# The forget gate of a two-layer decoder kernel as eight float32 products on column tiles

## Chip, core and metric

One core of a Trainium2 chip runs the whole kernel. The metric is the device time of one execution in microseconds (us). TensorE (PE) multiplies, VectorE (DVE) and ScalarE (ACT) copy, scale and reduce, GpSimd (POOL) does small things on the side, and SyncE (SP) issues nearly all DMAs. PE's clock has two levels, 1.2 and 2.4 GHz; the granted clock in the rows is a share of the higher one.

## What is computed

Two pre-norm layers over 256 tokens of width 1024: forgetting attention, then block-sparse attention, each followed by a SwiGLU feed-forward part and a gated embedding. The change touches the entry of the first layer:

```python
u = _rmsnorm(h, attn_norm_g[i])
proj = u @ fox_w_in[j]                      # (256, 3 * 1024 + 16)
q, k, v = _heads(proj[..., :D]), _heads(proj[..., D:2 * D]), _heads(proj[..., 2 * D:3 * D])
f_logit = proj[..., 3 * D:].astype(jnp.float32) + fox_b_f[j].astype(jnp.float32)
log_f = jax.nn.log_sigmoid(f_logit).transpose(0, 2, 1)
o = _fox_attention(q, k, v, log_f)          # logits get cumsum(log_f)[t] - cumsum(log_f)[s]
```

The sixteen columns at the end of `proj`, one per head, are the forget gate.

## The kernel before

Every large product is made three times, from operands split into a high part in float32r and the rest: hi by hi, hi by lo, lo by hi (`mm3`, lines 90 to 92). Weights come in tiles of 128 partitions by 1024 columns (512 KB, `half` and `blocks`). Each goes through three steps: SP's DMA into `raw` (six buffers), ACT's copy into `whi` (line 149), DVE's difference into `wlo` (line 150). Then PE uses it in about 2.7 us. The activations are split in the same way by `Norm.block` (line 183 on ACT, 184 on DVE) into `g`, times the norm's gain but without the norm's factor for each token. That factor is applied to the results.

The first layer's attention begins with the value stage (`attention`, loop over `c`): eight weight tiles k = 0 to 7, one for each 128 rows of the width, twelve products of 512 columns each, into four PSUM banks `v`. The first tile is taken in an order of its own (`enter`, line 382), since its halves come in one after the other. Tiles 1 and 2 share a DMA buffer `hw` with pieces of x; the other pieces come in `hw[:, 2]`.

After k = 3 the gate is made (`mid`, that is `fox_bias`): its weights `wf32`, copied four times side by side and split into `fh` and `fl`, take 24 products into the bank `pf`. Then ACT squares the residual in four parts (`square`, line 199), DVE and POOL turn the sums into the factor of each token (`root`, `col`), two products with an identity spread that factor over all partitions (`spread`, line 217, bank `pr`), and ACT and DVE copy it out (lines 220 and 221). ACT also issues three small DMAs here (`small`, line 285). `rest`, which is called behind the value stage, makes the logarithm and the running sum out of `pf`. The later norms call `spread` three more times.

The program is written in the order of the sources and scheduled by the framework: it sets for each engine one fixed order, and semaphores release the instructions in it. Each engine works off its own order.

Some tiles are laid out with gaps (`ENTRY`, `gapped`): where a new group of products begins, either DVE's difference is cut in two pieces or the first block stands apart from the rest.

Of the kernel before, what the change touches and what calls it, by code (L numbers as in the profile page):

```python
# [27 lines left out]
F32 = mybir.dt.float32  # L28
# [4 lines left out]
P = 128  # L33
# [38 lines left out]
def trunk(ctx: ExitStack, tc: tile.TileContext, x, xg, wx, xr, pt, w, cst, gf, rel, hot, rvm, out):  # L72
# [15 lines left out]
    def mm3(o, a, b, start, stop):  # L88
        (ah, al), (bh, bl) = a, b
        mm(o, ah, bh, start=start, stop=False, skip_group_check=True)  # L90
        mm(o, ah, bl, start=False, stop=False, skip_group_check=True)  # L91
        mm(o, al, bh, start=False, stop=stop, skip_group_check=True)  # L92


    first_line = one.tile([P, 32], F32, name="first_line")
# [27 lines left out]
    def half(at=0, entry=0):  # L123


        i = state["next"]
        state["next"] += 1
        if i not in (1, 2):
            raw = work.tile([P, HW + LINE], F32, tag="raw", bufs=RAW, name=f"raw{i}")
        ht, lt = (work.tile([P, HW + 2 * LINE], F32R, tag=n, bufs=6, name=f"{n}{i}") for n in ("whi", "wlo"))  # L130
        hi, lo = ht[:, at:at + HW], lt[:, at:at + HW]
        if entry:
            nc.sync.dma_start(raw[:, 0:HW], w[i - 2][:, 0:HW])
            nc.scalar.activation(hi, raw[:, 0:HW], AF.Copy)  # L134
            ats = [(at + FURTHER, 0, entry), (at + LINE, entry, HW)]
            for a, c0, c1 in ats:
                nc.vector.tensor_tensor(lt[:, a + c0:a + c1], raw[:, c0:c1], f32(hi[:, c0:c1]), op=ALU.subtract)  # L137
            return hi, [lt[:, a + k * P:a + (k + 1) * P] for a, c0, c1 in ats for k in range(c0 // P, c1 // P)]
        if i in (1, 2):
            raw = hw[:, i - 1, S:]  # L140
        parts = 2 if i < 2 else 1
        for q in range(parts):
            c = slice(q * HW // parts, (q + 1) * HW // parts)
            if i in (1, 2):
                at = slice(c.start + (S if q else 0), c.stop + S)
# [26 lines left out]
    class Norm:  # L172
# [39 lines left out]
        def spread(self, scale=1.0):  # L212

            n = self.n
            pr = bank(f"pr{n}")
            for t in range(2):
                mm(pr[:, t * P:(t + 1) * P], self.col[:, t:t + 1].to_broadcast([P, P]), ident,
                   start=True, stop=True)
            self.row = work.tile([P, 2, S], F32, tag="row", name=f"row{n}")
            nc.scalar.activation(self.row[:, 0], pr[:, 0:S], AF.Copy, scale=scale)  # L220
            nc.vector.tensor_copy(self.row[:, 1], pr[:, 0:S])
# [2 lines left out]
            return self.hi[:, m], self.lo[:, m]  # L224

    nm = Norm(0)
    nm.block(0, hx[0])
    first = [half()]
    for k in range(1, 4):
        first.append(half())  # L230
        if k < 3:
            nm.block(k, hx[k])
    nc.sync.dma_start(hw[:, 2], xr)
    for k in range(3, KT):
        nm.block(k, hx[k])
# [25 lines left out]
    def tokens(o, x, t, w, start, stop):  # L261

        at = slice(t * P, (t + 1) * P)
        mm3(o, (x[0][:, at], x[1][:, at]), w, start, stop)

    def pair_unit(bks, c, wt, x, ts=(0, 1), mid=None):

# [14 lines left out]
    def small(after):  # L282
        with tc.issue_after(after.ins):
            for t, a in ((rl, rel), (ht, hot), (rm, rvm)):
                nc.scalar.dma_start(t, a)
        table_parts()


    def fox_bias(nm):

        ft, lt = (work.tile([P, HW + 2 * LINE], F32R, tag=t, bufs=6, name=n) for n, t in (("fh", "whi"), ("fl", "wlo")))

        def four(t, at, k0, k1):
            return t[:, at + k0 * P:at + k1 * P].rearrange("p (k r c) -> p k r c", r=4, c=2 * H)

        n = len(ENTRY)
        fh = four(ft, APART, 0, KT)
        fl = [four(lt, APART + FURTHER, 0, n), four(lt, APART + LINE, n, KT)]  # L300
        for t in (fh, *fl):
            nc.gpsimd.memset(f32(t)[:, :, :, H:], 0.0)
        w4 = wf32.unsqueeze(2).to_broadcast([P, KT, 4, H])
        nc.scalar.activation(fh[:, :, :, 0:H], w4, AF.Copy)
        for t, k0, k1 in ((fl[0], 0, n), (fl[1], n, KT)):
            nc.vector.tensor_tensor(t[:, :, :, 0:H], w4[:, k0:k1], f32(fh[:, k0:k1, :, 0:H]), op=ALU.subtract)
        cols = [[t[:, k].rearrange("p r c -> p (r c)") for t in ts for k in range(t.shape[1])] for ts in ((fh,), fl)]
        pf = bank("pf")
        for k in range(KT):
            mm3(pf[:, :S], [t[k] for t in cols], nm.k(k),  # L310
                start=(k == 0), stop=(k == KT - 1))

        def rest():
            f = one.tile([P, S], F32, name="f")
            nc.vector.tensor_tensor(f, pf[:, :S], nm.row[:, 1], op=ALU.mult)
# [20 lines left out]
            return (lambda i: (mask[:, P:], mask)), add  # L336

        return rest

    def table_parts():  # L340
# [33 lines left out]
        return spread, load, (at, None)  # L374


    def enter(bks, x, w):

        for hf in range(2):
            for a, b in ((0, 0), (1, 0), (0, 1)):  # L380
                for t in range(2):
                    mm(bks[2 * t + hf], x[a][:, t * P:(t + 1) * P], w[b][:, hf * HC:(hf + 1) * HC],
                       start=a == b, stop=False, skip_group_check=True)

    def attention(layer, nm, mid, early, nf):
        vb = [bank(f"v{layer}_{b}") for b in range(4)]
        rest = None
        for c in range(4):
            wt = [early.pop(0) if early else half() for _ in range(2)]
            for kk in range(2):  # L390
                hi, lo = wt[kk]
                k = 2 * c + kk
                if layer == 1 and k == 3:
                    nm.turn(1)
                    nm.square(1)
                if early and k == 0:
                    enter(vb, nm.k(0), wt[0])
                    continue
                for t in range(2):
                    for hf in range(2):  # L400
                        cols = slice(hf * HC, (hf + 1) * HC)
                        tokens(vb[2 * t + hf], nm.k(k), t, (hi[:, cols], lo[:, cols]), k == 0, k == KT - 1)
# [24 lines left out]
        pq = {}  # L427

        def project(j, a):
            if j > 2 and j % 2 == 0 and a == 0:  # L430
# [459 lines left out]
```

## Time and profile before

| what | value |
|---|---|
| median of 3 runs (lowest, highest) | 655.08 us (654.88, 655.27) |
| the profiled execution, its span | 654.99 us, 653.0 us |
| PE busy | 644.5 us, 99% |
| DVE, ACT, POOL busy | 438.7, 376.4, 10.2 us |
| mean share of the DMA engines from 5.4 to 30 us, and after | 0.98 to 1.03, then 0.56 |
| granted PE clock over the span | 0.997 |

The span runs from the first to the last instruction; the run's time has some 2 us around it. A busy PE does not mean that it moves at its best: the ends of matmuls are modelled, so it is the starts that are to be read. Starts that follow each other at the shortest distance mean a full PE.

### The profile page before, as it was taken

The page shows a single profiled execution, that of the slowest core. Times are in us where ns is not written, and L with a number is a line of the kernel's source. Part 1 is how long each engine was busy: PE and PEld are TensorE (multiplying, and loading weights), DVE is VectorE, ACT ScalarE, POOL GpSimd, SP SyncE. Part 2 cuts the span into 40 slices and gives each one's busy share as a digit, 9 for nine tenths or more (in the row PEclk, how much of TensorE's full clock was granted, in tenths as well). Part 3 has the DMA queues.
Part 4 walks back from the last instruction along what each step waited for, and adds up shares of the span by engine and source line. Part 5 has one row for each costly group of instructions (what it writes and reads, how often), then busy time and mean ns, then how long its engine had stood idle before and what let it go on. Part 6 is the DMA issues. An engine that isn't in the chain of part 4 may idle for free.

```text
span 653.0 us, 11639 instructions
## 1 busy us (share of the span) xinstructions
PE 644.5 (99%) x4587; PEld 590.9 (90%) x4587; DVE 438.7 (67%) x717; ACT 376.4 (58%) x654; POOL 10.2 (2%) x24
## 2 busy tenths in 40 slices
PE   9999999999999999999999999999999999999995
PEld 7899988999999999998889999889999999999885
DVE  5788875586666666667675788666666666666665
ACT  7876675664444445448665677756544444454663
POOL 1100000000000000000000000000000000000000
PEclk9999999999999999999999999999999999999998
DMA  9969534286556556565586554344765665665501
GB/s 335 369 231 306 186 126 152 82 266 196 194 186 200 190 189 214 193 191 187 192 291 197 172 174 142 111 148 139 228 194 189 194 197 189 196 209 193 190 0 65
DMA packets 36085, 124.14 MB, mean 190 GB/s; under 512 B 3936, under 2 KB 6208, under 8 KB 36032
## 3 DMA queue, kind: packets, MB, share of 16 engines
q1 hardware_dynamic: 35552, 122.85, 57.3%
q8 instruction: 36, 0.59, 0.3%
q10 hardware_dynamic: 480, 0.55, 0.2%
q14 instruction: 17, 0.14, 0.1%
HBM read 122.32 MB, written 4.22 MB: 194 GB/s over the span
## 4 chain that ended last, share of the span: by engine, by line
PE 95%; issue 3%; DMA 1%; ACT 0%; POOL 0%; DVE 0%; POOLq 0%
PE gu L90 12%; PE gu L91 12%; PE gu L92 12%; PE fo L91 6%; PE fo L90 6%; PE fo L92 6%; PE pq L90 5%; PE pq L91 4%; PE pq L92 4%; PE wo L90 2%; PE wo L92 2%; PE wo L91 2%; PE v L91 2%; PE v L92 2%; PE v L90 2%
## 5 line engine op out<-in xcount | busy, mean ns | idle before, releaser
L150 DVE TENSOR_TENSOR wlo<-raw,whi 128x1024 fp32r<-128x1024 f32 (+1 forms) x187 | 227.4, 1220 | 118.6 <-ACT whi L149 117.0
L149 ACT ACTIVATE whi<-raw 128x1024 fp32r<-128x1024 f32 (+1 forms) x187 | 195.7, 1053 | 143.1 <-PE gu L91 46.2
L90 PE MATMUL gu<-g,whi 128*128 128x256 f32 x704 | 195.2, 277 | 0.0
L92 PE MATMUL gu<-g,wlo 128*128 128x256 f32 x704 | 194.8, 277 | 0.0
L91 PE MATMUL gu<-g,whi 128*128 128x256 f32 x704 | 194.8, 277 | 0.0
L90 PEld LDWEIGHTS gu<-g,whi 128*128 128x128 f32 x704 | 132.2, 188 | 0.8
L91 PEld LDWEIGHTS gu<-g,whi 128*128 128x128 f32 x704 | 132.2, 188 | 0.8
L92 PEld LDWEIGHTS gu<-g,wlo 128*128 128x128 f32 x704 | 132.4, 188 | 0.0
L90 PE MATMUL pq<-g,whi 128*128 128x256 f32 x256 | 71.5, 279 | 0.0
L92 PE MATMUL pq<-g,wlo 128*128 128x256 f32 x256 | 70.9, 277 | 0.0
L91 PE MATMUL pq<-g,whi 128*128 128x256 f32 x256 | 70.9, 277 | 0.0
L90 PE MATMUL fo<-whi,fp 128*128 128x512 f32 x176 | 68.9, 391 | 0.0
L91 PE MATMUL fo<-wlo,fp 128*128 128x512 f32 x176 | 68.7, 390 | 0.0
L92 PE MATMUL fo<-whi,fp 128*128 128x512 f32 x176 | 68.5, 389 | 0.0
L90 PEld LDWEIGHTS pq<-g,whi 128*128 128x128 f32 x256 | 48.1, 188 | 0.6 <-issue 0.2
L92 PEld LDWEIGHTS pq<-g,wlo 128*128 128x128 f32 x256 | 48.2, 188 | 0.0
L91 PEld LDWEIGHTS pq<-g,whi 128*128 128x128 f32 x256 | 48.1, 188 | 0.0
L258 ACT ACTIVATE fp<-sg 128x256 fp32r<-128x256 f32 x44 | 18.2, 418 | 48.5 <-DVE sg L611 48.5
L137 DVE TENSOR_TENSOR wlo<-raw,whi 128x256 fp32r<-128x256 f32 (+1 forms) x40 | 26.1, 688 | 23.7 <-ACT whi L134 23.7
L92 PEld LDWEIGHTS fo<-whi,fp 128*128 128x128 f32 x176 | 33.0, 188 | 7.0
L90 PEld LDWEIGHTS fo<-whi,fp 128*128 128x128 f32 x176 | 33.0, 188 | 6.3
L91 PEld LDWEIGHTS fo<-wlo,fp 128*128 128x128 f32 x176 | 33.0, 188 | 6.0
(156 smaller groups left out, 900.7 us busy)
## 6 DMA issues: line engine op xcount, KB each, us to landing
raw<-w SPq DMA_DIRECT2D x205, 512.0 KB, 3.6
raw<-w SPq DMA_DIRECT2D x8, 540.0 KB, 3.8
d<-d SPq DMA_DIRECT2D x4, 768.0 KB, 9.8
bias<-d SPq DMA_DIRECT2D x4, 512.0 KB, 5.1
h<-x SPq DMA_DIRECT2D x2, 512.0 KB, 9.4
out<-end SPq DMA_DIRECT2D x3, 256.0 KB, 2.0
hw<-wx SPq DMA_DIRECT2D x1, 640.0 KB, 6.5
hw<-xr SPq DMA_DIRECT2D x1, 640.0 KB, 8.3
```

The source lines that it names most:

```text
L90: mm(o, ah, bh, start=start, stop=False, skip_group_check=True)
L91: mm(o, ah, bl, start=False, stop=False, skip_group_check=True)
L92: mm(o, al, bh, start=False, stop=stop, skip_group_check=True)
L137: nc.vector.tensor_tensor(lt[:, a + c0:a + c1], raw[:, c0:c1], f32(hi[:, c0:c1]), op=ALU.subtract)
L149: nc.scalar.activation(hi[:, c], raw[:, c], AF.Copy)
L150: nc.vector.tensor_tensor(lo[:, c], raw[:, c], f32(hi[:, c]), op=ALU.subtract)
L258: nc.scalar.activation(hi, src, AF.Copy)
```

## The change

It makes the gate in float32, without the split: the weights are multiplied by the gain once (`wg`), and each of the eight products takes 32 columns of weights (16 of them zero) against a piece of x as it came in. Product k goes to the 32 partitions (k mod 4) of `pf`, so that four products use four different column tiles of PE, and the second four add to the first. ACT copies the bank out (`quarters`), and one more float32 product with `add4`, ones where rows belong to one head, sums the four quarters into `fsum`. This product and the spreading stand behind k = 5 now. The spreading products become transposes. The first hi copies (the first half of tiles 0 and 1, all of tile 2) go from ACT to DVE, with `nm.block` called inside `half`. `enter` is used for k = 1 too, in another order of its products. In layer 1 one more tile gets its difference in two pieces in place of a gap.

```diff
@@ half
-        for q in range(parts):
-            c = slice(q * HW // parts, (q + 1) * HW // parts)
+        cs = [slice(q * HW // parts, (q + 1) * HW // parts) for q in range(parts)]
+        for c in cs:
...
-            nc.scalar.activation(hi[:, c], raw[:, c], AF.Copy)
+        for c in cs:
+            if i < 3 and c.start == 0:
+                nc.vector.tensor_copy(hi[:, c], raw[:, c])
+                nm.block(i, hx[i])
+            else:
+                nc.scalar.activation(hi[:, c], raw[:, c], AF.Copy)
             nc.vector.tensor_tensor(lo[:, c], raw[:, c], f32(hi[:, c]), op=ALU.subtract)
@@ Norm.spread
-                mm(pr[:, t * P:(t + 1) * P], self.col[:, t:t + 1].to_broadcast([P, P]), ident,
-                   start=True, stop=True)
+                nc.tensor.transpose(pr[:, t * P:(t + 1) * P], self.col[:, t:t + 1].to_broadcast([P, P]), ident)
@@ fox_bias
-        fh = four(ft, APART, 0, KT)
-        fl = [four(lt, APART + FURTHER, 0, n), four(lt, APART + LINE, n, KT)]
...
-        nc.scalar.activation(fh[:, :, :, 0:H], w4, AF.Copy)
...
+        wg = work.tile([P, KT, 2 * H], F32, tag="sg", name="wg")
+        nc.gpsimd.memset(wg[:, :, H:], 0.0)
+        nc.vector.tensor_tensor(wg[:, :, 0:H], wf32, gn[:, 0, :].unsqueeze(2).to_broadcast([P, KT, H]), op=ALU.mult)
+        add4 = work.tile([P, 2 * S], F32, tag="fp", bufs=4, name="add4")[:, 0:P]
+        nc.gpsimd.tensor_copy(add4.rearrange("p (r h) -> p r h", h=H), sel32.unsqueeze(1).to_broadcast([P, P // H, H]))
         pf = bank("pf")
         for k in range(KT):
-            mm3(pf[:, :S], [t[k] for t in cols], nm.k(k),
-                start=(k == 0), stop=(k == KT - 1))
+            at = slice(k % 4 * 32, k % 4 * 32 + 32)
+            mm(pf[at, :S], wg[:, k], hx[k], start=k < 4, stop=k >= 4, skip_group_check=True)
+        quarters = work.tile([P, S], F32, tag="sg", name="quarters")
+        nc.scalar.activation(quarters, pf[:, :S], AF.Copy)
+        pf = []
+
+        def gather():
+            pf.append(bank("fsum"))
+            mm(pf[0][:, :S], add4, quarters, start=True, stop=True)
@@ attention
-                if early and k == 0:
-                    enter(vb, nm.k(0), wt[0])
+                if layer == 0 and k < 2:
+                    enter(vb, nm.k(k), wt[k], k == 0)
...
                 nm.root()
-                nm.spread(-0.125)
                 small(done)
+            if layer == 0 and c == 2:
+                with tc.issue_after(got.ins):
+                    nm.spread(-0.125)
+                    rest.gather()
...
-                hi, lo = blocks(ENTRY if j == 2 * layer and a == 0 else ())
+                hi, lo = blocks(ENTRY if j in ((0,), (2, 4))[layer] and a == 0 else ())
```

PE, behind the last product of k = 3, before (the first three of the gate's 24 products; `pr` spreads the factor, `whi_263` and `wlo_264` are the tile of k = 4):

```order
L92 MATMUL v_3_155<-whi_118,g_87 128x512
L90 MATMUL pf<-g_87,fh 128x256
L91 MATMUL pf<-g_87,fh 128x256
L92 MATMUL pf<-g_87,fl 128x256
...
L217 MATMUL pr_250<-con,col_248 128x128 x2
L90 MATMUL v_0_152<-whi_263,g_87 128x512
L90 MATMUL v_1_153<-whi_263,g_87 128x512
L90 MATMUL v_2_154<-whi_263,g_87 128x512
L90 MATMUL v_3_155<-whi_263,g_87 128x512
L91 MATMUL v_0_152<-wlo_264,g_87 128x512
```

The same place after; `whi_240` and `wlo_241` are the tile of k = 4 now, `whi_246` that of k = 5, `whi_284` that of k = 6:

```order
L92 MATMUL v_3_155<-whi_118,g_87 128x512
L300 MATMUL pf<-gx,wg 32x256
L300 MATMUL pf<-hw,wg 32x256 x7
L90 MATMUL v_0_152<-whi_240,g_87 128x512
L90 MATMUL v_1_153<-whi_240,g_87 128x512
L91 MATMUL v_0_152<-wlo_241,g_87 128x512
...
L92 MATMUL v_3_155<-whi_246,g_87 128x512
L222 MATMUL pr_275<-con,col_231 128x128 x2
L307 MATMUL fsum<-quarters,add_207 128x256
L90 MATMUL v_0_152<-whi_284,g_87 128x512
```

Eight products stand in place of 24, the spreading and the sum come two tiles later, and at k = 4 two products instead of four stand ahead of the first that reads wlo.

ACT, from the squares to the copies of k = 4 and k = 5, before (`sq` are the squares, `rl`, `ht` and `rm` the small DMAs):

```order
L199 ACTIVATE sq_0_1_241,ss_88<-h 128x512
L199 ACTIVATE sq_1_1_243,ss_88<-h 128x512
L285 DMA rl<-rel 64x16
L285 DMA ht<-hot 64x384
L285 DMA rm<-rvm 16x384
L149 ACTIVATE whi_263<-raw_262 128x1024
L149 ACTIVATE whi_269<-raw_268 128x1024
L220 ACTIVATE row_253<-pr_250 128x256
```

ACT at the same place after:

```order
L204 ACTIVATE sq_0_1_224,ss_88<-h 128x512
L302 ACTIVATE quarters<-pf 128x256
L204 ACTIVATE sq_1_1_226,ss_88<-h 128x512
L284 DMA rl<-rel 64x16
L284 DMA ht<-hot 64x384
L284 DMA rm<-rvm 16x384
L154 ACTIVATE whi_240<-raw_239 128x1024
L154 ACTIVATE whi_246<-raw_245 128x1024
```

The copy of the gate's bank, which reads what PE's eight products write, stands ahead of the last square, the DMA issues and the copies for k = 4 and k = 5; the copy of the spread factor no longer stands right behind these.

DVE at the first tiles, before (`whi_110` and `wlo_111` are the tile of k = 2, `wlo_119` that of k = 3):

```order
L150 TENSOR_TENSOR wlo_111<-hw,whi_110 128x1024
L184 SCALAR_TENSOR_TENSOR g_87<-hw,gx,g_87 128x256
L150 TENSOR_TENSOR wlo_119<-raw_117,whi_118 128x1024
L184 SCALAR_TENSOR_TENSOR g_87<-hw,gx,g_87 128x256 x5
```

DVE there after:

```order
L151 CAST whi_110<-hw 128x1024
L189 SCALAR_TENSOR_TENSOR g_87<-hw,gx,g_87 128x256
L155 TENSOR_TENSOR wlo_111<-hw,whi_110 128x1024
L155 TENSOR_TENSOR wlo_119<-raw_117,whi_118 128x1024
L189 SCALAR_TENSOR_TENSOR g_87<-hw,gx,g_87 128x256
```

The copy of tile 2 is DVE's now, and the difference of g comes between it and the difference of the weights.

## Rows read from the trace of the kernel before

**Rows 1.** The page's first section: PE's busy time, share of the span, instructions.

```profile
PE 644.5 (99%) x4587; PEld 590.9 (90%) x4587; DVE 438.7 (67%) x717; ACT 376.4 (58%) x654; POOL 10.2 (2%) x24
```

**Rows 2.** Waits of PE: who waited for whom, us in total, times, longest.

```profile
PE v L382 <- ACT whi L149: 0.7, 1, 0.7
```

**Rows 3.** Timeline at k = 2: start, length, engine, line, operation, out<-in, count.

```profile
9.06 1.06 ACT L149 ACTIVATE whi<-hw 128x1024 fp32r<-128x1024 f32 x1 [0.91 <-DMA hw<-wx]
...
10.16 1.23 DVE L150 TENSOR_TENSOR wlo<-hw,whi 128x1024 fp32r<-128x1024 f32 x1 [1.27 <-ACT whi L149]
...
11.46 0.71 PE L91 MATMUL v<-wlo,g 128*128 128x512 f32 x2
...
12.83 2.07 DVE L184 SCALAR_TENSOR_TENSOR g<-hw,gx,g 128x256 fp32r<-128x256 f32 x5
```

**Rows 4.** Timeline of PE at the gate, and to the start of k = 6.

```profile
16.55 0.28 PE L90 MATMUL pf<-g,fh 128*128 128x256 f32 x1
...
19.31 0.60 PE L217 MATMUL pr<-con,col 128*128 128x128 f32 x4
19.67 1.17 PE L90 MATMUL v<-whi,g 128*128 128x512 f32 x4
20.67 0.39 PE L91 MATMUL v<-wlo,g 128*128 128x512 f32 x1
...
22.49 0.39 PE L90 MATMUL v<-whi,g 128*128 128x512 f32 x1
...
25.21 0.39 PE L90 MATMUL v<-whi,g 128*128 128x512 f32 x1
```

**Rows 5.** Timeline of PE: transposes, then float32 products on 64-column tiles.

```profile
82.77 0.82 PE L497 MATMUL pp<-con,e 128*128 128x128 f32 x6
83.52 1.08 PE L511 MATMUL po<-pt,v 128*64 128x256 f32 x8
84.43 0.61 PE L513 MATMUL po<-pt,v 128*64 128x128 f32 x8
```

**Rows 6.** Timeline of ACT, its DMA issues (ACTq), and one row of DVE.

```profile
0.74 0.41 ACTq L115 DMA_DIRECT2D gx<-xg  x1
...
1.19 1.28 ACT L102 ACT_TABLE_LOAD   x1 [1.19 <-PEq L882]
...
14.91 0.19 ACT L199 ACTIVATION_READ_ACCUMULATOR sq<-h 128x1 f32 x1
...
15.14 0.53 ACTq L285 DMA_DIRECT2D rl<-rel  x1
...
16.30 0.62 ACT L199 ACTIVATE sq<-h 128x512 f32<-128x512 f32 x1
...
16.34 0.60 ACTq L285 DMA_DIRECT2D rm<-rvm  x1
...
16.99 2.02 ACT L149 ACTIVATE whi<-raw 128x1024 fp32r<-128x1024 f32 x2
...
18.09 2.36 DVE L150 TENSOR_TENSOR wlo<-raw,whi 128x1024 fp32r<-128x1024 f32 x2 [0.68 <-ACT whi L149]
...
19.95 0.39 ACT L220 ACTIVATE row<-pr 128x256 f32<-128x256 f32 x1 [0.94 <-PE pr L217]
```

**Rows 7.** Groups by line: the spreading products (busy us, mean ns, idle).

```profile
L217 PE MATMUL pr<-con,col 128*128 128x128 f32 x16 | 2.4, 274 | 0.0
```

**Rows 8.** Timeline at the first products of the feed-forward part's second half.

```profile
137.73 0.76 DVE L259 TENSOR_TENSOR fp<-sg,fp 128x256 fp32r<-128x256 f32 x2
...
139.86 0.39 PE L92 MATMUL fo<-whi,fp 128*128 128x512 f32 x1
```

**Rows 9.** Stretches: length, busy us of each engine, PEclk, DMA share, GB/s.

```profile
0.70:3.85 3.15, 3.08 (x7) 2.51 (x8) 0.00 (x0) 1.49 (x2) 1.35 (x6) 1.00 0.62 187
...
645.70:648.90 3.20, 0.31 (x3) 0.11 (x2) 2.04 (x8) 1.90 (x4) 0.55 (x1) 1.00 0.27 105
...
648.97:653.00 4.03, 0.00 (x0) 0.00 (x0) 0.48 (x1) 0.45 (x1) 0.00 (x0) 0.50 0.44 170
```

More of the change, by code (lines that the diff above doesn't have):

```diff
@@ L91, in mm3 @@
         mm(o, ah, bl, start=False, stop=False, skip_group_check=True)
-        mm(o, al, bh, start=False, stop=stop, skip_group_check=True)
+        return mm(o, al, bh, start=False, stop=stop, skip_group_check=True)
     first_line = one.tile([P, 32], F32, name="first_line")
@@ L141, in half @@
         parts = 2 if i < 2 else 1
-        for q in range(parts):
-            c = slice(q * HW // parts, (q + 1) * HW // parts)
+        cs = [slice(q * HW // parts, (q + 1) * HW // parts) for q in range(parts)]
+        for c in cs:
             if i in (1, 2):
-                at = slice(c.start + (S if q else 0), c.stop + S)
+                at = slice(c.start + (S if c.start else 0), c.stop + S)
                 nc.sync.dma_start(hw[:, i - 1, at], wx[i - 1][:, at])
@@ L226, in trunk @@
     nm = Norm(0)
[L227 to L232, printed above, removed]
+    first = [half() for _ in range(4)]
     nc.sync.dma_start(hw[:, 2], xr)
@@ L263, in tokens @@
         at = slice(t * P, (t + 1) * P)
-        mm3(o, (x[0][:, at], x[1][:, at]), w, start, stop)
+        return mm3(o, (x[0][:, at], x[1][:, at]), w, start, stop)
     def pair_unit(bks, c, wt, x, ts=(0, 1), mid=None):
@@ L289, in fox_bias @@
     def fox_bias(nm):
[L293 to L298, printed above, removed]
-        fh = four(ft, APART, 0, KT)
-        fl = [four(lt, APART + FURTHER, 0, n), four(lt, APART + LINE, n, KT)]
-        for t in (fh, *fl):
-            nc.gpsimd.memset(f32(t)[:, :, :, H:], 0.0)
-        w4 = wf32.unsqueeze(2).to_broadcast([P, KT, 4, H])
-        nc.scalar.activation(fh[:, :, :, 0:H], w4, AF.Copy)
-        for t, k0, k1 in ((fl[0], 0, n), (fl[1], n, KT)):
-            nc.vector.tensor_tensor(t[:, :, :, 0:H], w4[:, k0:k1], f32(fh[:, k0:k1, :, 0:H]), op=ALU.subtract)
-        cols = [[t[:, k].rearrange("p r c -> p (r c)") for t in ts for k in range(t.shape[1])] for ts in ((fh,), fl)]
+        wg = work.tile([P, KT, 2 * H], F32, tag="sg", name="wg")
[3 more added lines that the diff above has]
+        nc.gpsimd.tensor_copy(add4.rearrange("p (r h) -> p r h", h=H), sel32.unsqueeze(1).to_broadcast([P, P // H, H]))
         pf = bank("pf")
         for k in range(KT):
-            mm3(pf[:, :S], [t[k] for t in cols], nm.k(k),
-                start=(k == 0), stop=(k == KT - 1))
+            at = slice(k % 4 * 32, k % 4 * 32 + 32)
[6 more added lines that the diff above has]
+            mm(pf[0][:, :S], add4, quarters, start=True, stop=True)
         def rest():
             f = one.tile([P, S], F32, name="f")
-            nc.vector.tensor_tensor(f, pf[:, :S], nm.row[:, 1], op=ALU.mult)
+            nc.vector.tensor_tensor(f, pf[0][:, :S], nm.row[:, 1], op=ALU.mult)
             nc.vector.tensor_scalar(f, f, bfs, None, op0=ALU.add)
@@ L336, in rest @@
             return (lambda i: (mask[:, P:], mask)), add
+        rest.gather = gather
         return rest
@@ L374, in moba_bias, with enter @@
         return spread, load, (at, None)
[L377 to L383, printed above, removed]
+    def enter(bks, x, w, start):
+        for hf, a, b in [(hf, a, 0) for hf in range(2) for a in range(2)] + [(0, 0, 1), (1, 0, 1)]:
+            for t in range(2):
+                mm(bks[2 * t + hf], x[a][:, t * P:(t + 1) * P], w[b][:, hf * HC:(hf + 1) * HC],
+                   start=start and a == b, stop=False, skip_group_check=True)
     def attention(layer, nm, mid, early, nf):
@@ L401, in attention @@
                         cols = slice(hf * HC, (hf + 1) * HC)
-                        tokens(vb[2 * t + hf], nm.k(k), t, (hi[:, cols], lo[:, cols]), k == 0, k == KT - 1)
+                        got = tokens(vb[2 * t + hf], nm.k(k), t, (hi[:, cols], lo[:, cols]), k == 0, k == KT - 1)
             if layer == 0 and c == 1:
@@ L429, in project @@
         def project(j, a):
-            if j > 2 and j % 2 == 0 and a == 0:
+            if j > 2 + 2 * layer and j % 2 == 0 and a == 0:
                 hi, lo = gapped()
             else:
-                hi, lo = blocks(ENTRY if j == 2 * layer and a == 0 else ())
+                hi, lo = blocks(ENTRY if j in ((0,), (2, 4))[layer] and a == 0 else ())
             if a == 0:
@@ L838 @@
         seq += _rows(wi[:, 2 * D:3 * D])
-        seq += [_gapped(a) if n % 4 == 0 and n > 4 else a for n, a in enumerate(_cols(wi[:, :D], wi[:, D:2 * D]))]
+        seq += [_gapped(a) if n % 4 == 0 and n > 4 + 4 * i else a for n, a in enumerate(_cols(wi[:, :D], wi[:, D:2 * D]))]
         seq += [_wide(wo, 2 * c, hf) for hf, c in ((0, 0), (1, 0), (0, 1), (1, 1), (0, 2), (1, 2), (0, 3), (1, 3))]
```

## The prediction

> **What bounds the kernel now.** I read the page's first section, then what TensorE (PE) waited for, then the order of time of each engine between 4 and 26 us, where the change lies. PE is busy for 644.5 of 653.0 us [rows 1], and in the whole run its products wait for an operand once, before the first product of the value stage [rows 2]. From there on it goes from product to product, one of 512 columns every 0.227 us: eight take the 1.82 us between 20.67 and 22.49 [rows 4]. So a microsecond that PE gains or loses early goes to the end, since nothing later waits and could give it back. The one question is whether the operands still come in time where the products go.
>
> **The change, part by part.** I follow PE through the value stage, whose weight tiles k = 0 to 7 take 12 products each, and give each place as after minus before. The profiled execution took 654.99 us, its span 653.0; the median shown is 655.08, so both bases agree to 0.1 us, and I add to 654.99.
>
> *First tiles.* VectorE (DVE) now makes the first hi copies, so the first product may start up to half a microsecond sooner. That is lost again at k = 2. Its weights land at 9.06, where ScalarE (ACT) begins its copy; DVE's difference follows at 10.16, lasts 1.23, and the first wlo product comes at 11.46 [rows 3], 0.07 behind its end. After, DVE does it all in a row: copy, g difference, wlo. No row has this copy. The nearest are ACT's of the same tile, 1.06 us [rows 3], and DVE's difference over as many columns, 1.13 from one to the next (2.36 - 1.23) [rows 3, 6]; I take 1.13, DVE's own pace. Five g differences take 2.07, 0.41 each [rows 3]. So wlo ends at 9.06 + 1.13 + 0.41 + 1.23 = 11.83 instead of 11.39: **+0.44**. The bounds: a copy as long as one whole difference, 1.23, makes it +0.54; from below, a copy of no length ends wlo at 10.70, PE itself, if it starts at about 5.0 and makes 26 products by then, comes there at 11.0, so -0.5. The Trainium skill (VectorE: DVE Perf Modes, section Mode 2×_2P — use both read ports for one tensor) has it that a float32 copy from SBUF to SBUF takes two elements a cycle. No row here shows that; with about 0.53 for the copy, as an estimate from that page, every sum below would be 0.6 us lower, and the forecast 656.8.
>
> *Gate products.* Before, 24 products fill 16.55 to 19.31 (2.76 us), and the two spreading products come behind them, to 19.67 [rows 4]. After, eight float32 products stand there. A float32 product is two instructions (the two of a spread show as x4). On two 64-column tiles eight such instructions, 256 columns wide, took 0.91 us, from 83.52 to 84.43, and 1.08 to the end of the last [rows 5]: two at a time, 0.23 a round. Four 32-column tiles are not in the trace; four at a time make four rounds and again 1.08, two at a time eight rounds, 0.91 more. I take the first, since tiles of one product each did overlap, plus 0.10 for entering the tiled form. The gate then ends at 16.55 + 0.44 + 0.10 + 1.08 = 18.17. For PE alone this is a gain of about 1.7 us.
>
> *Who waits for that.* ACT's order now has the copy "quarters" of that bank ahead of the last square, three DMA issues and the copies of k = 4 and k = 5. All of these were free of PE before: the copy of k = 4 started at 16.99 [rows 6], under the gate's products, and that cover is gone. ACT saw PE's spreading product 0.04 after its end (19.31 + 0.60, 19.95) [rows 4, 6], so quarters starts at 18.21. The DMA issues: before, the first came at 15.14, just when the last square had what it waits for (the first one's buffer, of three, free with the accumulator read that ends at 14.91 + 0.19 = 15.10), although two squares had still to start; from it to the end of the third issue it is 1.80 us (16.34 + 0.60 - 15.14), and the next copy starts 0.05 later, at 16.99 [rows 6]. I read this as: a waiting instruction holds what is behind it, DMA issues too, and the issues hold the copy. The table load that starts at 1.19, behind the issue of 0.74 to 1.15, reads the same way [rows 6]. So the copy of k = 4 starts at 18.21 + 0.04 + 1.80 + 0.05 = 20.10, ends 1.06 later (two take 2.02, 0.96 apart), and PE gets it at 21.21. Its first wlo is another 1.23 on DVE: 21.19 to 22.42, and 0.07 to PE, 22.49. PE stands still from 18.2 to 21.2 and, after two products, again for 0.8 (22.49 - 21.21 less two at 0.23).
>
> *At k = 4.* Before, the first wlo product started at 20.67 with eight of the twelve left, and k = 5 began at 22.49 [rows 4]. After, it starts at 22.49 with ten left (the new order has two products ahead of it): ten at 0.227, plus 0.09 for starting behind a wait (the four of 19.67 take 1.00 until 20.67 in place of 0.91 [rows 4]) end at 24.85. **+2.36** in all.
>
> *Spread and sum, now behind k = 5.* Two transposes at 0.11 (six lie 0.11 apart: (0.82 - 0.27) / 5, with 0.27 for one [rows 5, 7]) and the product with ones, two rounds of 0.23: 0.68. k = 6 would start at 24.85 + 2.72 + 0.68 = 28.25, against 25.21: **+3.04**. ACT and DVE have k = 5 to 7 ready by then at 1.0 and 1.13 us a tile against PE's 2.72.
>
> *Later.* Sixteen spreading instructions become eight [rows 7]; four of them are in the sums above, the other three spreads each lose two at 0.11: **-0.66**. In the feed-forward part DVE's order puts one wlo (1.13) ahead of the products' first sg; fp's lo now ends at 137.73 + 0.76 = 138.49 and is wanted at 139.86 [rows 8], so 1.37 of slack less 1.13 and less the 0.22 that PE gains just before: next to nothing left, nothing lost; up to 0.2 in each layer otherwise. The other cut of one weight tile in layer 1 I take as 0, +-0.1. The memsets and copies on POOL end by 14 us, three us ahead of their use: 0.
>
> Sum: 3.04 - 0.66 = +2.38, so **657.4 us**.
>
> **The rivals.**
> 1. *The clock falls as well.* At the end of the run PE has 0.31 us of work in 3.2 us (645.70 to 648.90), and from 648.97 on the granted clock is 0.50, that is 1.2 GHz [rows 9]. The stretch worked out above is as thin: nothing for 3.0 us, then two products, then 0.8 of nothing. If the clock falls there, the price is that of the warm-up: seven products in 3.15 us [rows 9], 0.45 each for 0.227 (the pace of the lower level, though the column reads 1.00 there), so half of a stretch of about 3.1 us less the part in which PE waits anyway (0 to 0.8): 1.2 to 1.6. It would give 658.8. Against it: the fall in the trace came behind the last product, with no work following.
> 2. *The DMA issues don't hold the copy.* Then only the engine's work does: quarters 0.39, the last square to the copy 0.69 (16.30 to 16.99) [rows 6]: the copy starts at 19.29 instead of 20.10, all is 0.81 earlier, 656.6. With the first tiles at their lower bound it would be 655.7, which is no longer told from no change. The Trainium skill (Perfetto Trace Analysis, section DVE / Act Engine Instruction (TENSOR_ADD, Activation, etc)) supports it: an instruction that waits stands in a queue of its own, and the sequencer goes on to the next. By that rule the three DMAs would be issued while quarters waits, and the forecast would be 656.6; the 15.14 right behind 15.10 speaks for the other reading.
> 3. *The tiles don't do what the change says.* Two at a time: 0.91 more, 658.3; the two-tile rows speak against it.
> 4. *Not slower.* If the copy of k = 4 runs under the gate's products as before, PE waits only for its wlo, 18.09 + 1.23, and takes it at 19.39; ten products from there, +0.09, end at 21.75, 0.74 ahead of before. With 0.68 for spread and sum and -0.66 later this is 654.3. It decides from the point where the copy starts before about 18.9 us. Against it stands ACT's order, in which nothing lets that copy pass quarters.
>
> **How the numbers follow.** The forecast has 0.40 (656.7 to 658.0), the clock 0.28, the free DMA issues 0.17, two at a time 0.07, not slower 0.08. The range goes from 655.8, which takes in rival 2 down to about its lower bound, to 659.2, the clock's fall with its dearer price, and leaves out the last rival and the tails, some 2 in 10. A measurement of this kernel tells 0.2% from no change, 1.3 us, so "same" is 653.8 to 656.4: most of rival 4, and of rival 2 what lies below its 656.6, together 0.17. Faster needs rival 4 and a microsecond more: 0.05. Slower: 0.78.
>
> **What would show it.** The list of what PE waited for should have a new entry of about 3 us, the first product of k = 4 waiting for ACT's copy, and one of 0.6 to 0.8 for DVE's wlo. On ACT, quarters should start about 0.04 behind the last gate product, at 17.6 to 18.3, with the three DMA issues behind it and the copy right after the third; if the copy begins before that, rival 2 holds. The eight gate products should fill about 1.0 us; 1.9 would be rival 3. The granted clock between 20 and 26 us tells rival 1. DVE's copy of 1024 columns shows its own length. k = 6 should start near 28.2. The forecast is wrong if PE's wait ahead of k = 4 is under 1.5 us, or if the later 600 us change by more than the 0.66.

## The result and the profile after

The changed kernel takes 659.70 us (median of 6 runs, 659.14 to 660.44) against 655.02 (6 runs, 654.88 to 655.36) on the same chip: 1.0070 times as long, 95% interval 1.0059 to 1.0081. So it is slower, as forecast, but by 4.7 us and not by 2.3, and 0.5 us above the range. The six runs fall into two groups, three at 659.1 to 659.2 and three at 660.2 to 660.4, whose mean granted clocks over the span are 0.995 and 0.992. The median lies between the groups, and no run came near it. The profiled execution took 660.41 (span 658.5), so it is one of the longer ones.

The page's first section, the answer to [rows 1]: PE still covers 98% of the span, but a busy PE was not one at its pace.

```profile
PE 647.6 (98%) x4573; PEld 591.8 (90%) x4573; DVE 439.8 (67%) x720; ACT 373.7 (57%) x651; POOL 10.7 (2%) x23
```

What PE waited for (who for whom, us, times, longest), where [rows 2] had one wait of 0.7:

```profile
PE v L90 <- ACT whi L154: 3.0, 1, 3.0
```

PE from the gate to the first products of k = 6 (start, length, line, what, and in brackets the wait ahead of it), the answer to [rows 4]:

```profile
16.87 0.40 PE L300 MATMUL pf<-gx,wg 128*32 128x256 f32 x1
16.88 0.42 PE L300 MATMUL pf<-hw,wg 128*32 128x256 f32 x3
17.11 0.38 PE L300 MATMUL pf<-gx,wg 128*32 128x256 f32 x1
17.12 0.82 PE L300 MATMUL pf<-hw,wg 128*32 128x256 f32 x11
20.98 1.22 PE L90 MATMUL v<-whi,g 128*128 128x512 f32 x2 [3.04 <-ACT whi L154]
22.24 0.80 PE L91 MATMUL v<-wlo,g 128*128 128x512 f32 x1
...
23.25 0.63 PE L91 MATMUL v<-wlo,g 128*128 128x512 f32 x1
23.68 0.63 PE L92 MATMUL v<-whi,g 128*128 128x512 f32 x1
...
26.67 0.60 PE L90 MATMUL v<-whi,g 128*128 128x512 f32 x1
...
29.67 0.38 PE L222 MATMUL pr<-con,col 128*128 128x128 f32 x2
29.88 0.60 PE L307 MATMUL fsum<-quarters,add 128*128 128x256 f32 x2
30.13 0.58 PE L90 MATMUL v<-whi,g 128*128 128x512 f32 x1
30.55 0.39 PE L91 MATMUL v<-wlo,g 128*128 128x512 f32 x1
```

ACT in the same stretch (ACTq are its DMA issues), the answer to [rows 6]:

```profile
18.01 0.38 ACT L302 ACTIVATE quarters<-pf 128x256 f32<-128x256 f32 x1 [1.66 <-PE pf L300]
18.02 0.53 ACTq L284 DMA_DIRECT2D rl<-rel  x1
18.29 0.62 ACT L204 ACTIVATE sq<-h 128x512 f32<-128x512 f32 x1
18.59 0.60 ACTq L284 DMA_DIRECT2D ht<-hot  x1
...
19.23 0.60 ACTq L284 DMA_DIRECT2D rm<-rvm  x1
19.87 3.90 ACT L154 ACTIVATE whi<-raw 128x1024 fp32r<-128x1024 f32 x4 [0.87 <-issue]
```

Stretches of the span (from:to, length, busy us of PE, PEld, DVE, ACT, POOL, then PEclk, DMA share, GB/s), cut where the granted clock changes:

```profile
6.64:20.29 13.65, 11.30 (x62) 8.59 (x60) 8.14 (x16) 8.13 (x19) 1.43 (x3) 1.00 1.03 417
20.29:23.70 3.41, 2.69 (x6) 1.69 (x7) 2.74 (x3) 3.41 (x5) 0.43 (x1) 0.50 0.67 223
23.70:27.12 3.42, 3.42 (x10) 2.68 (x9) 3.42 (x4) 1.96 (x3) 2.80 (x3) 0.50 0.82 259
```

The chain that was forecast is there link by link: gate, quarters, the three issues, the copy of k = 4, 3.0 us of an idle PE. New is the last column but two: from 20.29 to 27.12 the granted clock is 0.50, 1.2 GHz. Products that follow each other every 0.227 us at full clock start 0.43 apart (23.25, 23.68). None of the shorter runs was traced; their mean clock of 0.995 and their 1.2 us less suggest a fall about half as long.

### The profile page after: what moved, and what is told of

Read it like the earlier page. It is cut to its first block, busy times and chain, and to the rows that moved or that the text cites. A ratio compares the mean times of both kernels' runs of the same rounds, so it can differ in the third digit from the quotient of the medians.

```text
span 658.5 us, 11610 instructions
## 1 busy us (share of the span) xinstructions
PE 647.6 (98%) x4573; PEld 591.8 (90%) x4573; DVE 439.8 (67%) x720; ACT 373.7 (57%) x651; POOL 10.7 (2%) x23
## 4 chain that ended last, share of the span: by engine, by line
PE 95%; issue 3%; ACT 0%; POOL 0%; ACTq 0%; DVE 0%; POOLq 0%
PE gu L92 12%; PE gu L90 12%; PE gu L91 12%; PE fo L90 6%; PE fo L91 6%; PE fo L92 6%; PE pq L90 5%; PE pq L91 4%; PE pq L92 4%; PE wo L90 2%; PE wo L92 2%; PE wo L91 2%; PE v L90 2%; PE v L91 2%; PE v L92 2%
## 5 line engine op out<-in xcount | busy, mean ns | idle before, releaser
L137 DVE TENSOR_TENSOR wlo<-raw,whi 128x256 fp32r<-128x256 f32 (+1 forms) x42 | 27.9, 701 | 25.4 <-ACT whi L134 25.4
```

## The experiments

All times are medians; the kernel before, run beside each group, gave 655.02 to 655.10.

| run | us | against before (95% interval) |
|---|---|---|
| changed kernel | 659.70 | 1.0070 (1.0059 to 1.0081) |
| e1_late_quarters | 656.04 | 1.0017 (1.0008 to 1.0026) |
| e2_filler | 657.50 | 1.0038 (1.0024 to 1.0051) |
| e3_small_late | 657.95 | 1.0043 (1.0030 to 1.0055) |
| e4_transposes_alone | 655.23 | 1.0003 (0.9994 to 1.0012) |
| e5_sum_behind_k4 | 655.08 | 0.9998 (0.9989 to 1.0007) |
| e6_hi_first_k4 | 654.79 | 0.9996 (0.9987 to 1.0005) |
| e7_hi_first_products | 654.48 | 0.9991 (0.9983 to 1.0000) |
| e8_transposes_entry | 654.81 | 0.9998 (0.9989 to 1.0007) |
| e9_transposes_twice | 655.47 | 1.0005 (0.9996 to 1.0014) |
| e10_copies_on_act | 654.37 | 0.9989 (0.9980 to 0.9998) |

**What held PE: e1.** In the changed kernel, ACT's copy of the gate's bank is written where the sum is made:

```diff
+        gate, pf = pf, []
         quarters = work.tile([P, S], F32, tag="sg", name="quarters")
-        nc.scalar.activation(quarters, pf[:, :S], AF.Copy)
-        pf = []
 
         def gather():
+            nc.scalar.activation(quarters, gate[:, :S], AF.Copy)
             pf.append(bank("fsum"))
```

> The changed kernel with one thing moved: ACT's copy quarters now stands behind the copies of k = 4 and k = 5 instead of ahead of the last square. Theory (ACT's order holds the copy of k = 4 until PE is through with the gate; PE then stands still 3 us and its clock falls): the copy of k = 4 starts near 17.1 us instead of 19.87, PE waits once for wlo only, 0.5 to 1.2 us instead of 3.0, the granted clock stays at 1.00 from 7 us on, k = 6 starts within 0.3 us of before's 25.2, and the time is about 655.3 (654.6 to 656.0). Rival A (the three DMA issues or the late landing of x hold the copy, not quarters): the copy starts at 18.5 or later, PE waits over 2 us, 657.5 to 660. Rival B (the clock falls because of the 16 short products on column tiles, not because of the wait): half clock from about 20 us all the same, 656.5 to 658.

656.04 us (11 runs, 655.32 to 657.63). ACT of this kernel, PE at k = 4 and the waits of PE that it still has:

```profile
16.78 2.01 ACT L154 ACTIVATE whi<-raw 128x1024 fp32r<-128x1024 f32 x2
18.69 0.36 ACT L305 ACTIVATE quarters<-pf 128x256 f32<-128x256 f32 x1
...
25.66 1.06 ACT L154 ACTIVATE whi<-raw 128x1024 fp32r<-128x1024 f32 x1 [1.36 <-DMA raw<-w]
26.63 0.36 ACT L224 ACTIVATE row<-pr 128x256 f32<-128x256 f32 x1
```

```profile
17.89 0.73 PE L90 MATMUL v<-whi,g 128*128 128x512 f32 x2 [0.43 <-ACT whi L154]
19.15 0.50 PE L91 MATMUL v<-wlo,g 128*128 128x512 f32 x1 [0.53 <-DVE wlo L155]
...
24.77 0.58 PE L90 MATMUL v<-whi,g 128*128 128x512 f32 x1
```

```profile
PE sp L459 <- DVE qkl L258: 0.6, 1, 0.6
PE v L91 <- DVE wlo L155: 0.5, 1, 0.5
PE v L90 <- ACT whi L154: 0.4, 1, 0.4
```

The copy of k = 4 starts at 16.78, no wait is over 0.6, the clock stays full, and k = 6 starts at 24.77, ahead of the 25.21 of [rows 4]. One line in ACT's order was worth 3.7 us. The rivals A and B are out: the three issues still stand ahead of that copy, and the sixteen short products are still there. But the time was 0.7 above the 655.3 that I expected, just over the upper end of 656.0, and part of that is a new wait: the first scores wait 0.6 us for qkl. The copy of the spread factor stands on ACT behind a weight copy that waits 1.36 us for its DMA, and the forget gate's exponential and the running sum come behind it; that this chain makes the wait is tried in e5.

**What the clock cost: e2.** The changed kernel with thirteen products of zeros on PE between the gate and k = 4.

```diff
-        quarters = work.tile([P, S], F32, tag="sg", name="quarters")
+        filler = bank("filler"); [mm(filler, still.to_broadcast([P, P]), still.to_broadcast([P, 512]), start=True, stop=True) for _ in range(13)]; quarters = work.tile([P, S], F32, tag="sg", name="quarters")
```

> The changed kernel with 13 products of zeros with zeros, 512 columns each, into a bank that nobody reads, put on PE between the gate's products and k = 4: they fill about 3 us in which PE otherwise waits. Theory (the fall of the granted clock between 20 and 27 us comes from the wait and costs 1.1 to 2.3 us by itself): clock 1.00 throughout, the copy of k = 4 where it was (19.9), first wlo product at about 22.25, products from there 0.227 apart, k = 6 near 27.9 to 28.0, time 657.9 to 658.3, the spread of 1.2 us between executions gone. Rival (the products from 22 to 27 us are slow for another reason, such as the stretch in which DMAs, ACT and DVE all write at once): clock share 0.50 or not, products 0.43 apart, 659.1 to 660.5 as in the changed kernel.

657.50 us, all five runs within 0.3, and 0.4 below the lower end of what I expected. PE, and the stretch that was at half clock in the changed kernel:

```profile
17.67 3.11 PE L301 MATMUL filler<-const-float32-0.0 128*128 128x512 f32 x13
20.77 1.17 PE L90 MATMUL v<-whi,g 128*128 128x512 f32 x4
22.03 0.50 PE L91 MATMUL v<-wlo,g 128*128 128x512 f32 x1
```

```profile
20.30:27.10 6.80, 6.72 (x30) 4.92 (x29) 6.35 (x6) 5.17 (x6) 2.47 (x3) 1.00 0.81 272
```

With PE occupied the clock stays at 1.00, products come 0.23 apart, and the two groups of runs are gone. So the fall came from the wait. Not all of the 1.7 and 2.9 us against the two groups is the clock: the scheduler put four whi products ahead of the first wlo here, not two (two at 0.227, 0.45), and in the profiled executions wlo came 0.2 earlier, as the whole start did. That leaves 2.3 us for the longer group, whose trace says the same: some 11.4 products between 22.24 and 27.12 at 0.427 instead of 0.227 are 2.3 us. For the shorter group it leaves about 1.0, if its runs started like the profiled one, which no trace shows.

**The three DMA issues: e3.**

```diff
                 nm.root()
-                small(done)
             if layer == 0 and c == 2:
                 with tc.issue_after(got.ins):
                     nm.spread(-0.125)
                     rest.gather()
+                small(got)
```

> The changed kernel with the three small DMAs (and what POOL makes of them) issued by ACT behind the copies for k = 6 on, instead of ahead of the copy of k = 4; quarters stays where it is. Theory (the issues hold the copy, 0.9 us): the copy of k = 4 starts right behind the last square at 18.95 to 19.05 instead of 19.87, PE's wait falls from 3.0 to about 2.1 us; at full clock that is 656.7, with one stretch of half clock 657.8, with two 659.0. Rival (the issues cost nothing, the copy waits for something else): copy at 19.8 or later, 659.1 to 660.5.

657.95 us (656.74 to 658.45).

```profile
18.29 0.62 ACT L204 ACTIVATE sq<-h 128x512 f32<-128x512 f32 x1
...
18.90 2.94 ACT L154 ACTIVATE whi<-raw 128x1024 fp32r<-128x1024 f32 x3
```

```profile
20.00 1.86 PE L90 MATMUL v<-whi,g 128*128 128x512 f32 x4 [2.06 <-ACT whi L154]
```

```profile
20.28:23.70 3.41, 3.41 (x9) 2.62 (x9) 3.41 (x4) 2.93 (x4) 0.00 (x0) 0.50 1.03 377
```

The copy follows the square at once, 0.97 us earlier, so the issues did hold it. PE's wait is 2.1 us, and the clock falls for 3.4 us only; it falls at 20.28, when the wait has been over for 0.28 us (here too four whi products come first). One of the five runs has a mean clock of 0.997 where the profiled one has 0.994, and it is the 656.74, 1.2 us below the median: a fall of 3.4 us costs about that. The profiled execution points to about 1.0: its five products from the first wlo on take 2.10 us (21.65 to 23.75) where five at 0.227 take 1.14.

**The pace behind the later spreads: e4, e8, e9.** With the starts of equal products in the two traces side by side, PE's lag changed in six places behind k = 6, where I had expected three gains of 0.22: -0.23, +0.31, -0.23, +0.40, -0.23, +0.31 us. The gains are the three spreads. The losses lie in the weight tiles right behind them, and nothing waits there. Two products 45 places apart in the first such stretch, of before and of after:

```profile
132.25 0.28 PE L90 MATMUL gu<-g,whi 128*128 128x256 f32 x1
...
137.35 0.28 PE L90 MATMUL gu<-g,whi 128*128 128x256 f32 x1
```

```profile
137.18 0.28 PE L90 MATMUL gu<-g,whi 128*128 128x256 f32 x1
...
142.48 0.28 PE L90 MATMUL gu<-g,whi 128*128 128x256 f32 x1
```

5.10 us for 45 products before, 0.113 each, and 5.30 after, 0.118 each. These products go at one of two paces here, and keep it over tens of products. The kernel before has slow stretches too (from about 120 to 131 us, for one), and there the spread ended it. e4 is the kernel before with transposes in the four spreads and nothing else:

```diff
-                mm(pr[:, t * P:(t + 1) * P], self.col[:, t:t + 1].to_broadcast([P, P]), ident,
-                   start=True, stop=True)
+                nc.tensor.transpose(pr[:, t * P:(t + 1) * P], self.col[:, t:t + 1].to_broadcast([P, P]), ident)
```

> The kernel before with the four spreads as transposes and nothing else changed. Theory (two instructions fewer in each spread, 0.22 us, but after the three later ones PE goes through the next 256-column products at 0.118 us in place of 0.113 until it meets products of another shape, which loses 0.31, 0.40 and 0.31 us): four times -0.22 and +1.02, 655.1 to 655.3, no change. Rival (the prediction's: each spread just loses 0.22 us; the slower pace in the changed kernel has another cause): 654.1 to 654.2.

655.23 us, no change, and the losses of its trace behind the three later spreads are +0.31, +0.40 and +0.31: the theory held. e8, which like e9 has the transposes of e4, gives the tiles behind those spreads the layout of the tuned tiles at group starts (`ENTRY`: the difference in two pieces, the second 56 columns further):

```diff
...
-                hi, lo = blocks(ENTRY if j == 2 * layer and a == 0 else ())
+                hi, lo = blocks(ENTRY if j in ((0,), (0, 2))[layer] and a == 0 else ())
...
-                if fs[0] == 2 and a:
-                    wt = gapped()
-                else:
-                    wt = blocks(ENTRY if fs[0] % 2 == 0 and a == 0 and fs[0] > 2 else ())
+                wt = blocks(ENTRY if fs[0] % 2 == 0 and a == 0 and fs[0] > 2 or fs[0] == 2 and a else ())
...
-        a[0], a[5] = _gapped(a[0], 3), _gapped(a[5])
+        a[0] = _gapped(a[0], 3)
```

> The kernel before with all spreads as transposes, and the weight tile that follows each of the three later spreads laid out as the tuned tiles at group starts are (wlo in two pieces, the second 56 columns further) instead of with a gap or without one. Theory (the slower pace is a state that the layout of the next tile can end as the two instructions more did): products behind the later spreads 0.118 apart for the first five or so and 0.113 from there, 654.2 to 654.5. Rival (the pace is set by the transposes themselves and lasts until another shape comes, whatever the layout): as the transposes alone, 655.1 to 655.4.

And e9 makes each transpose twice, so that four instructions stand there again:

```diff
-                mm(pr[:, t * P:(t + 1) * P], self.col[:, t:t + 1].to_broadcast([P, P]), ident,
-                   start=True, stop=True)
+                for _ in range(2):
+                    nc.tensor.transpose(pr[:, t * P:(t + 1) * P], self.col[:, t:t + 1].to_broadcast([P, P]), ident)
```

> The kernel before with each spread's two transposes made twice, so that four PE instructions stand there as before the change. Theory (what counts for the pace behind the spread is the number of instructions or their time on PE): 0.113 us a product behind all spreads, 655.0 to 655.2, as before. Rival (the kind of instruction sets the pace): 0.118 behind the three later spreads, 1.02 more, 656.0 to 656.2.

654.81 us for e8 and 655.47 for e9, each between its theory and its rival. The products that fit into the same stretches (count in the first brackets) of the kernel before, of e4, e8 and e9, in this order; the two lines of each are the first layer's feed-forward part and the second layer's attention:

```profile
132.00:138.00 6.00, 6.00 (x55) 6.00 (x54) 6.00 (x11) 4.87 (x8) 0.00 (x0) 1.00 0.89 282
352.00:361.00 9.00, 9.00 (x82) 9.00 (x81) 5.65 (x6) 4.06 (x5) 0.00 (x0) 1.00 0.64 203
```

```profile
132.00:138.00 6.00, 6.00 (x53) 6.00 (x52) 5.78 (x11) 4.19 (x7) 0.00 (x0) 1.00 0.89 293
352.00:361.00 9.00, 9.00 (x79) 9.00 (x78) 5.63 (x6) 4.00 (x5) 0.00 (x0) 1.00 0.66 202
```

```profile
132.00:138.00 6.00, 6.00 (x54) 6.00 (x53) 6.00 (x10) 4.20 (x7) 0.00 (x0) 1.00 0.87 305
352.00:361.00 9.00, 9.00 (x82) 9.00 (x81) 5.77 (x7) 4.41 (x5) 0.00 (x0) 1.00 0.64 194
```

```profile
133.00:139.00 6.00, 6.00 (x55) 6.00 (x54) 6.00 (x13) 4.72 (x8) 0.00 (x0) 1.00 0.85 286
352.00:361.00 9.00, 9.00 (x79) 9.00 (x78) 5.27 (x7) 4.36 (x5) 0.00 (x0) 1.00 0.63 194
```

Neither theory holds everywhere. The layout of e8 restores the pace in the attention tile (82) and not in the two feed-forward tiles (54, and by the starts of its products each loses 0.30). Four instructions instead of two restore it in both feed-forward tiles (55) and not in the attention tile (79). So the pace depends on what PE did just before and on the layout of the next weights, and not on transposes alone; which property of these decides is open.

**Mending it: e5, e6, e7, e10.** Each goes on from the one before it, beginning with e1. e5 sets spread and sum behind k = 4:

```diff
+                if layer == 0 and k == 4:
+                    with tc.issue_after(got.ins):
+                        nm.spread(-0.125)
+                        rest.gather()
...
-            if layer == 0 and c == 2:
-                with tc.issue_after(got.ins):
-                    nm.spread(-0.125)
-                    rest.gather()
```

> The kernel with quarters behind the copies, and besides the spread and the sum of the quarters right behind k = 4 instead of k = 5. Theory (with the wait at k = 4 gone, the next late thing is the chain from the sum through the forget gate's exponential on ACT to the first scores; the spread factor's copy on ACT stood behind a weight copy that waited for its DMA): the copy of the factor comes near 23 us instead of 26.6, the wait of the first scores for qkl (0.6 us) goes, the spread between executions shrinks, about 655.1 (654.8 to 655.5). Rival (that wait has another cause, such as the DMAs): still 0.4 us or more at the first scores, 655.7 to 656.5.

655.08 us, as expected. The factor's copy comes 3.2 us sooner than in e1, the wait of the first scores is gone, and the runs lie within 0.7:

```profile
23.45 0.37 ACT L224 ACTIVATE row<-pr 128x256 f32<-128x256 f32 x1
```

e6 takes k = 4 by `enter`, its eight whi products first (`enter` returns its last product now):

```diff
+                if layer == 0 and k == 4:
+                    with tc.issue_after(enter(vb, nm.k(k), wt[kk], False).ins):
+                        nm.spread(-0.125)
+                        rest.gather()
+                    continue
```

> As the one with the sum behind k = 4, and k = 4 takes its products in the order of the first tiles: the eight that read whi ahead of the four that read wlo. Theory: the wait of 0.5 us for wlo at k = 4 goes, the one of 0.4 us for the copy stays, 654.5 (654.2 to 654.9). Rival (the wait only moves to the next tile, since DVE's wlo of k = 5 comes no sooner): 655.0 to 655.3.

654.79 us, inside the theory's range: 0.29 less than e5, where 0.6 was expected. The wait for wlo went, but PE now comes to the first scores sooner than ACT and DVE do:

```profile
PE sp L461 <- DVE qkl L258: 0.4, 1, 0.4
PE v L378 <- ACT whi L154: 0.4, 1, 0.4
```

e7 keeps the transposes in the first spread alone:

```diff
-                nc.tensor.transpose(pr[:, t * P:(t + 1) * P], self.col[:, t:t + 1].to_broadcast([P, P]), ident)
+                if n:
+                    mm(pr[:, t * P:(t + 1) * P], self.col[:, t:t + 1].to_broadcast([P, P]), ident, start=True, stop=True)
+                else:
+                    nc.tensor.transpose(pr[:, t * P:(t + 1) * P], self.col[:, t:t + 1].to_broadcast([P, P]), ident)
```

> As the one with the eight whi products first, and only the first spread by transposes, the three later ones by products as in the kernel before. Theory (the transposes in the later norms lose more at the pace of the products behind them than the two instructions give): 0.2 to 0.4 us less than the one with four transposed spreads, 654.2; 256-column products behind the later spreads 0.113 apart. Rival (transposes are a gain of 0.22 us each): 0.66 more, 655.2.

654.48 us, 0.31 less, as expected. e10 puts `half` and the calls of `nm.block` back as they were before the change, so that ACT makes the first hi copies:

```diff
-            if i < 3 and c.start == 0:
-                nc.vector.tensor_copy(hi[:, c], raw[:, c])
-                nm.block(i, hx[i])
-            else:
-                nc.scalar.activation(hi[:, c], raw[:, c], AF.Copy)
+            nc.scalar.activation(hi[:, c], raw[:, c], AF.Copy)
...
```

> The fastest kernel so far (quarters and sum moved, whi products first at k = 4, later spreads as products) with the first hi copies back on ACT as in the kernel before. Theory (DVE's copy of 1024 columns takes 0.69 us, so that wlo of k = 2 is ready 0.6 us before it is wanted, and the copies on DVE bring the first product 0.2 to 0.6 us forward): 654.6 to 655.0, that is 0.1 to 0.5 slower. Rival (the prediction's step on the first tiles: the copies on DVE cost 0.44 us at k = 2): 0.44 faster, 654.0 to 654.1.

654.37 us: neither 0.1 to 0.5 slower nor 0.44 faster than e7, and 0.11 less lies inside the scatter. What the copies on DVE bring at the start (in e7 the first product comes at 5.17, in e10 at 5.30) is waited away at k = 4 in these two traces, where the copy comes when ACT is through with its squares: e7 waits 0.4 us there, e10 not at all. But the clock first rose at 5.42 us in e7 and at 6.45 in e10, so e10 came later to that place for another reason too; how much is the copies' stays open. This is the fastest kernel here, 0.7 us under before (0.9989, 0.9980 to 0.9998). Of the change it keeps the gate on four column tiles, the first spread by transposes, `enter` for k = 1 and the other cut of one tile in layer 1, and it takes k = 4 by `enter` besides; the later transposes, the copies on DVE and the places of quarters and sum are gone. What each of the kept parts is worth alone was not run.

## Why the prediction was right in direction and wrong in size

The steps of the prediction and what the changed kernel's profiled execution shows:

| step | predicted | measured |
|---|---|---|
| DVE's copy of 1024 columns | 1.13 us | 0.69 |
| first gate product, against before | +0.54 | +0.32 |
| the eight gate products | 1.08 us | 1.07 |
| quarters starts | 18.21 | 18.01 |
| copy of k = 4 starts | 20.10 | 19.87 |
| PE takes k = 4, its first wlo | 21.21, 22.49 | 20.98, 22.24 |
| from there to k = 5 (ten products) | 2.36 us | 4.43 |
| k = 5 starts | 24.85 | 26.67 |
| spread and sum | 0.68 us | 0.46 |
| k = 6 starts | 28.25 | 30.13 |
| from k = 6 to the end, against before | -0.66 | +0.51 |

**The step that failed first is "At k = 4", and with it the choice of the likeliest case.** It put ten products at 0.227 us and 0.09 for the start, 2.36 in all; they took 4.43, at 0.43 each and a granted clock of 0.50. "The clock falls as well" stood as a rival with 0.28. The argument against it, that the fall of [rows 9] came with no work following, was no reason that it could not come with work following. All six runs of the changed kernel have a lower mean clock, and e2 shows that the wait causes it. Up to the first wlo product every link is 0.2 to 0.25 early, by the start; behind it the measured chain loses 2.1 us on the predicted one and is 1.8 behind it at 26.67. The second wait that was forecast, 0.6 to 0.8 us for wlo, is not in the list of waits: at half clock the two whi products fill the time from 20.98 to 22.20.

**The rival's price was half right.** 1.2 to 1.6 us was worked out for a fall of about 3.1 us; one of 3.4 us cost about 1.0 to 1.2 (e3, and the shorter group against e2). But in the traced one of the three longer runs the clock was down for 6.83 us, which cost 2.3. With 0.28 at 658.8 and no case of a fall twice as long, the upper end of 659.2 was too low. The direction came by the chain that was forecast. The three shorter runs, 659.14 to 659.20, lie just inside the range, but by two causes that the likeliest case had at nothing, the clock and the pace.

**The term "Later" has the wrong sign.** Three spreads did lose 0.23 us each, a little over the -0.66. But products 0.118 apart in place of 0.113 cost 0.20 for 45 of them, and 0.31, 0.40 and 0.31 in the three whole stretches: a net of about +0.32 where -0.66 stood, 0.98 of the miss. e4 shows the same losses from the transposes alone; which property sets the pace stays open. The prediction looked for waits there (the slack at fo, the tile with the other cut) and was right that none came; it didn't ask whether PE would keep its pace. The other 0.19 of the +0.51 is the first product behind the sum: 0.42 us from 30.13 to 30.55, where 0.227 was reckoned. It belongs to spread and sum, which took 0.46 instead of 0.68: the product with ones took 0.25 (29.88 to 30.13), not 0.46, and with these 0.19 the term was nearly met, by luck.

**First tiles.** This step failed in its reason; that the gate came +0.32 late, where +0.54 was predicted, is luck. DVE's copy is short:

```profile
8.98 0.69 DVE L151 CAST whi<-hw 128x1024 fp32r<-128x1024 f32 x1 [0.16 <-DMA hw<-wx]
9.59 0.48 DVE L189 SCALAR_TENSOR_TENSOR g<-hw,gx,g 128x256 fp32r<-128x256 f32 x1
9.99 1.22 DVE L155 TENSOR_TENSOR wlo<-hw,whi 128x1024 fp32r<-128x1024 f32 x1
```

It takes 0.69, with 0.61 to the next start, and wlo ends at 11.21, 0.58 ahead of its first product (11.79). The Trainium skill's rule (VectorE: DVE Perf Modes, section Mode 2×_2P — use both read ports for one tensor), two elements a cycle, from which the prediction had its estimate of 0.53, came closer than DVE's own pace of 1.13. The +0.32 comes from the clock: in this execution it rose at 6.64 us and in that of before at 3.85, so the first twelve products took from 5.17 to 8.62, 3.44 us, against 2.88. In e1, which has the same first tiles and whose clock rose at 4.37, the gate starts at 16.39, 0.16 ahead of before: there the step has the other sign.

**Rival 2 fell.** The first issue starts 0.01 behind quarters' start, not while quarters waits; the copy starts 0.05 behind the end of the third; and e3, without the issues, starts it 0.97 earlier. The rule of the Trainium skill (Perfetto Trace Analysis, section DVE / Act Engine Instruction (TENSOR_ADD, Activation, etc)), that the sequencer goes on past a waiting instruction, would have put the issues ahead of 18.01; this trace does not agree with it.

**Rival 3 fell**: four instructions at a time start within 0.02 us, and the rounds are 0.24 (16.87 to 17.11) and 0.22. **Rival 4** is what e1 made true: with the copy of k = 4 at 16.78, ahead of the 18.9 that the rival named, k = 6 comes before its old time. But a time like its 654.3 came only with e7 and e10; e1 lost 0.9 at the first scores by the starts of the products, 0.6 of it in the wait shown above, and 0.3 to the pace.

## What to carry to other kernels

Before a product on PE is shortened, look for what its old length covered on the other engines, and in whose order the copy of its result will stand: here a copy that waits for PE, put ahead of weight copies that did not, cost more than the products saved. A PE wait like those seen here (2.1 and 3.0 us) is to be priced with the clock's fall behind it, and with a longer fall too (6.83 us beside 3.41). And where nothing waits, compare the starts of equal products: 4% of pace over 45 of them is worth nearly as much as a spread's two instructions.

## What the hardware showed that was not expected

- The granted clock fell to 0.50, that is 1.2 GHz, with work still to follow: at 20.29 us in the changed kernel, within a wait of PE that ended at 20.98, and at 20.28 in e3, 0.28 us behind the end of a wait of 2.06. It stayed there while products were running: for 6.83 us in the changed kernel's profiled execution, for 3.41 in that of e3. With the two waits of e1 (0.43 and 0.53) it stayed at 1.00.
- When the clock first rose differed between executions with the same ten products of warm-up, and moved the gate by half a microsecond: in before and e8, which are alike up to there, it rose at 3.85 and 6.89 us and the first gate product came at 16.55 and 17.02; in e1 and the changed kernel at 4.37 and 6.64, with the gate at 16.39 and 16.87.
- Products of 256 columns ran at 0.113 or at 0.118 us each (5.10 and 5.30 us for 45), with no wait and at full clock; the kernel before has such a slow stretch from about 120 to 131 us.
- Behind the float32 product with ones, the next product of 512 columns took 0.42 us to the one after it, nearly twice its 0.227, at full clock (30.13 to 30.55).
- ACT's DMA issues did not pass an instruction that waited: the first came 0.01 us behind the start of the copy that had waited 1.66 us for PE, and the three held the next weight copy 0.97 us (e3).
